# One expert stage gets another block order, and one entry of the load list becomes a barrier

## The chip, the cores and the metric

The kernel runs on one core of one Trainium2 chip. The metric is device time in microseconds (us), the median of several executions. One execution is also recorded by the hardware profiler; all rows below are from that one.

## The reference

The kernel computes a three-layer network on 256 tokens of width 1024, batch 1, all in float32. Layer one takes the tokens and 256 context tokens, mixes them by three kinds of attention and a gated linear scan, and ends in a mixture of experts: a router gives each token two of 32 experts, each with an up projection 1024 to 1024 (gate and value), a product with a sigmoid-weighted unit, and a down projection 512 to 1024. Then follow two layers of another kind (latent attention, stick-breaking attention, pooling), each with 32 experts of hidden width 256.

```
order = jnp.argsort(expert)                      # layer one: tokens sorted by expert
...
hid = jax.nn.silu(a) * b * combine[:, g, :, None]  # layers two and three, all experts, most weights 0
y = y + jnp.einsum('nef,efd->nd', hid, w_down[g])
```

Only experts that got tokens have to be computed, so how many tokens an expert has is known only at run time. The weights of the expert of layer one that has the fewest tokens weigh as much as those of the fullest: 6 MB.

## The kernel before, in words

Everything that is large comes from HBM through a ring of 22 SBUF slots of 1 MB (`RING`, class `Stream`). The order of the loads is a list, `S.specs`, written once by `stream_first` and `stream_rest`. `pump` takes entries from its head and issues one DMA on SyncE's queue (line L335) for each free slot; it is called at each `release` of a slot. A load whose address depends on the routing (`piece`, `get`) is not issued before the routing of its stage is known (`routes`). For all but the two fullest experts the DMA carries a condition, so that ranks with no tokens move nothing. Within the expert stages 20 slots serve the stream; the other two hold the split activations `hu` and `lu`. From the last block of a stage on, six freed slots are kept back for the next stage (`S.reserve(6)`, five in the last one).

An expert stage (`moe_phase`) is cut into blocks of 128 rows. Its plan (`_plan`) has static blocks (fixed experts, whose loads need no routing: experts 8 to 11 in stage one, two to a block), and rank blocks, whose experts are sorted by token count at run time: rank 0 gets two blocks ("wide", 256 rows, one set of weights), rank 1 one block, then pairs of experts with 64 rows each, then quads of four experts with 32 rows each. Whatever the order of the blocks, ranks keep their capacity. In stage one of the kernel before the order is

```
static static | rank0 rank0 rank1 | pair pair | quad quad quad quad quad
```

A block of n experts takes 6n MB of weights (4 up, 2 down), the second rank-0 block none. All blocks take the same rows through TensorE: n experts occupy n column groups side by side. In each turn p the loop runs `up(p)` (L1700, eight steps over the width), a gather of the group of blocks after (odd p only), the scatter of block p-2, `down(p-1)` (L1700 too) and a transposition of block p (L1724). Up slots are freed as the steps go on, down slots at the end of `down`.

After the last block come some statistics (`stats`, L1807 to L1829), and then a nest of branches (`nest`, L1847): rare routings need spare blocks, which lie inside the branches. In the recorded execution none is taken. Every engine runs through the branch. Then the next layer (`second_phase`) scales the tokens (L1920), transposes them (L1929), copies them (L1933, L1935) and projects them with six weight blocks `win2` (L1954); `prep` first splits each block into two halves on ScalarE and VectorE (L1903, L1907). Its loads stand in the list right behind the stage's last expert: `fg` (after stage one only), `win2` block 0, the constants `c2`, `win2` block 1, `wuq2`, `wsm2`, `win2` blocks 2 to 5, the rest of `c2`, four of `wout2`.

Of the kernel before, what the change touches and what calls it, by code (L numbers as in the profile page):

```python
# [33 lines left out]
SPARE = 16  # L34
# [5 lines left out]
        self.width = 128 // n  # L40


def _plan(start, statics, wide, wides, pairs, quads):
    blocks = [Block("static", start + wide * i, wide) for i in range(statics // wide)]
    lead = len(blocks)
    rank = 0
    for halves in wides:
        blocks += [Block("rank", rank, 1, 128 * i) for i in range(halves)]
        rank += 1
    cap = [128 * h for h in wides]  # L50
    for n, m in ((2, pairs), (4, quads)):
        for _ in range(m):
            blocks.append(Block("rank", rank, n))
            rank += n
            cap += [128 // n] * n
    main = len(blocks)
    blocks += [Block("rank", rank + 2 * i, 2, spare=True) for i in range(SPARE // 2)]
    return start, statics, lead, blocks, main, rank, cap


PLAN = {1: _plan(8, 4, 2, (2, 1), 2, 5), 2: _plan(8, 8, 4, (), 4, 4)}


def _layout_columns():
# [12 lines left out]
def _consts_main():  # L77
# [13 lines left out]
    for k in (1, 2):  # L91
        st0, ns, lead, _, _, nr, cap = PLAN[k]
        static = (e >= st0) & (e < st0 + ns)
# [205 lines left out]
class Stream:  # L299
# [14 lines left out]
    def add(self, src, dst=None):  # L314
        self.specs.append((src, dst))

    def pump(self):
        while self.specs:
            src, dst = self.specs[0]
            if dst is not None:  # L320
                self.nc.sync.dma_start(dst, src)
                self.specs.pop(0)
                continue
            if not self.free:
                return
            if callable(src):
                src = src()
                if src is None:
                    return
            cond = None  # L330
            if isinstance(src, tuple):
                src, cond = src
            self.specs.pop(0)
            u = self.unit(self.free.pop(0))
            self.nc.sync.dma_start(u.t[:, :src.shape[1]], src, **({} if cond is None else {"cond": cond}))  # L335
            self.ready.append(u)
# [30 lines left out]
def _flat(ap):  # L367
    n = len(ap.shape)
    if n == 2:
        return ap  # L370
    names = "abcd"[:n - 1]
    return ap.rearrange(f"p {' '.join(names)} -> p ({' '.join(names)})")
# [3 lines left out]
def hybrid_kernel(ctx: ExitStack, tc: tile.TileContext, A, out, dbg=None):  # L376
# [11 lines left out]
    def mark(label):  # L388
        if dbg is not None and "_mark" in dbg:
            dbg["_mark"](label)  # L390

    S = Stream(nc, ringp, range(RING - LENT - 1))
# [33 lines left out]
            S.add(_flat(A["wout"][u]))  # L426

    routes = {}

    def expert(R, u):  # L430
        if u not in R.regs:
            R.regs[u] = nc.values_load(R.info[0:1, u:u + 1], engines=[ENG.SP], min_val=0, max_val=31)
        return R.regs[u]

    def piece(key, src, blk, i, sub):
# [4 lines left out]
        def get():  # L440
# [6 lines left out]
            if "n" not in R.regs:  # L447
                nr = PLAN[key[0]][5]
                R.regs["n"] = nc.values_load(R.info[0:1, nr + SPARE + 1:nr + SPARE + 2], engines=[ENG.SP], min_val=0,
# [4 lines left out]
    def add_moe(key, ups, dns, nu, nd):  # L454
        _, _, lead, blocks, NL, _, _ = PLAN[key[0]]

        def add(p, src, n):
            if blocks[p].at:
                return
            for i in range(n):  # L460
                for e in range(blocks[p].n):
                    S.add(piece(key, src, blocks[p], e, (i,)))

        for p in range(NL + 1):
            if p < NL:
                add(p, ups, nu)
            if p > 0 and p != lead:
                add(p - 1, dns, nd)
            if p == lead - 1:
                add(p, dns, nd)  # L470

    def stream_rest():
        add_moe((1, 0), A["up1"], A["dn1"], 4, 2)
        S.add(A["fg"][0].to_broadcast([128, 1024]))
        for l in range(2):
            for b in range(6):
                S.add(_flat(A["win2"][l, b]))
                if b == 0:
                    S.add(A["c2"][:, 0:1792])
                if b == 1:  # L480
                    S.add(_flat(A["wuq2"][l]))
                    S.add(A["wsm2"][l])
            S.add(A["c2"][:, 1792:])
            for u in range(4):
                S.add(_flat(A["wout2"][l, u]))
            add_moe((2, l), A["gu2"][l], A["dn2"][l], 2, 1)
        S.add(A["fg"][1].to_broadcast([128, 1024]))
# [294 lines left out]
    def first_phase():  # L782
        with ExitStack() as es:
# [11 lines left out]
                               (A["wr1"], wrk.rearrange("p k e -> p (k e)")),  # L795
                               (A["br"].to_broadcast([128, 108]), brow.rearrange("p l e -> p (l e)"))])
            stream_rest()
            S.pump()
            def c1c(n):
# [634 lines left out]
    def moe_phase(kind, l, R, final=None):  # L1434
        _, _, lead, blocks, NL, NR, _ = PLAN[kind]
        NS = NR + SPARE
# [5 lines left out]
        with ExitStack() as es:  # L1442
# [318 lines left out]
            for p in range(NL + 1):  # L1761
                g = p // 2
# [97 lines left out]
            nest(NL)  # L1860
            if final is not None:
                S.release(fgu)
            mark("final")
            R.lu = S.unit(R.lu.slot)
            R.vrt = vrt
# [346 lines left out]

    R = first_phase()
    R = moe_phase(1, 0, R, 0)
    for l in range(2):
        R = second_phase(l, R)
        R = moe_phase(2, l, R, 1 if l == 1 else None)
# [22 lines left out]
```

## Time and profile before

| | us |
|---|---|
| median of 3 runs | 1468.6 (1467.32 to 1471.26) |
| the profiled execution | 1466.8 |
| its span | 1465.0 |
| TensorE busy | 1244.6 (85%) |
| VectorE / ScalarE / GpSimd busy | 433.7 / 341.8 / 98.3 |
| the load queue | 458.04 MB, 77.0% of the DMA engines' span |

Busy time on TensorE includes matmuls that run one after another while their weights arrive, so its share does not say which stage is limited by TensorE and which by loads; that is read stage by stage. Stage one's expert blocks lie between 299 and 739 us, those of the two later layers between about 895 and 1097 and between about 1255 and 1452 us.

### The profile page before, as it was taken

How to read it: one execution, taken by the hardware profiler on the slowest of the kernel's cores; microseconds unless marked ns; L12 is line 12 of the kernel's file. 1: busy time of each engine (PE TensorE's matmuls, PEld its weight loads, DVE VectorE, ACT ScalarE, POOL GpSimd, SP SyncE). 2: the span in 40 equal slices, each digit the busy share in tenths (PEclk: the TensorE clock that was granted, in tenths of full speed). 3: DMA queues.
4: the chain of work that ended last, by engine and by line, in shares of the span. 5: the costliest groups of instructions: out<-in, count | busy, mean ns of one | idle time of the engine just before them, and what ended most of it. 6: DMA issues, size and time to landing. Idle time of an engine off the chain costs nothing. (4 is left out here: it accounts for less than half of the span.)

```text
span 1465.0 us, 18831 instructions
## 1 busy us (share of the span) xinstructions
PE 1244.6 (85%) x7278; PEld 670.7 (46%) x7278; DVE 433.7 (30%) x1026; ACT 341.8 (23%) x709; POOL 98.3 (7%) x87
## 2 busy tenths in 40 slices
PE   5999999899999876767729998998672999899775
PEld 3778774544543311211218854443122875444211
DVE  5365443522212100100135524221012543422102
ACT  4431344211111100100035522211012552121102
POOL 1262100000000000000011100000000210000000
PEclk9999999999999988998969999999995999999998
DMA  8644329787689999999981458999996244899995
GB/s 343 259 174 158 144 69 421 261 336 292 246 330 386 421 421 421 420 421 422 421 328 66 179 191 336 420 421 421 421 421 260 98 203 185 341 421 421 421 421 205
DMA packets 64544, 459.47 MB, mean 314 GB/s; under 512 B 7408, under 2 KB 7728, under 8 KB 9904
## 3 DMA queue, kind: packets, MB, share of 16 engines
q1 hardware_dynamic: 64432, 458.04, 77.0%
q8 instruction: 63, 1.03, 0.3%
q14 instruction: 49, 0.40, 0.1%
HBM read 466.40 MB, written 1.05 MB: 319 GB/s over the span
## 5 line engine op out<-in xcount | busy, mean ns | idle before, releaser
L1700 PE MATMUL up<-ring,xg 128*32 128x512 f32 (+2 forms) x2016 | 381.5, 632 | 74.6 <-DMA ring<-in_up_dram 38.1
L1700 PEld LDWEIGHTS up<-ring,xg 128*32 128x32 f32 (+2 forms) x2016 | 105.8, 125 | 319.0 <-issue 180.4
L1700 PE MATMUL mm<-ring,hdT 128*32 128x512 f32 (+2 forms) x1008 | 199.6, 627 | 35.9 <-DMA ring<-in_dn_dram 34.4
L564 PE MATMUL ps<-ring,ring 128*128 128x256 f32 (+1 forms) x960 | 143.1, 306 | 1.3 <-POOL ring L897 0.6
L564 PEld LDWEIGHTS ps<-ring,ring 128*128 128x128 f32 x960 | 128.1, 191 | 20.0 <-issue 5.4
L1716 DVE TENSOR_TENSOR hd<-hd,up 128x256 f32<-128x256 f32 (+1 forms) x32 | 16.6, 520 | 393.3 <-ACT hd L1715 393.3
L1700 PEld LDWEIGHTS mm<-ring,hdT 128*32 128x32 f32 (+2 forms) x1008 | 53.4, 125 | 160.6 <-issue 89.7
L1715 ACT ACTIVATE hd<-up 128x256 f32<-128x256 f32 (+1 forms) x32 | 14.8, 464 | 400.3 <-PE up L1700 400.3
L1954 PE MATMUL ps<-ring,ring 128*128 128x256 f32 x384 | 52.1, 301 | 28.5 <-DVE ring L1935 28.5
L1515 PEld LDWEIGHTS mm<-P,ring 128*128 128x128 f32 x512 | 67.8, 202 | 12.6 <-issue 11.0
L1515 PE MATMUL mm<-P,ring 128*128 128x256 f32 x512 | 71.7, 298 | 0.8 <-DVE xg L1525 0.3
L1954 PEld LDWEIGHTS ps<-ring,ring 128*128 128x128 f32 x384 | 50.9, 208 | 29.5 <-ACT ring L1933 29.3
L599 PE MATMUL mm<-ring,ring 128*128 128x512 f32 (+1 forms) x192 | 64.1, 487 | 0.0
L1746 DVE SCALAR_TENSOR_TENSOR yl<-mm,gt,yh 128x512 fp32r<-128x512 f32 x40 | 30.0, 751 | 102.7 <-ACT yh L1745 102.7
L1745 ACT ACTIVATE yh<-mm,gt 128x512 fp32r<-128x512 f32 x40 | 27.5, 687 | 105.5 <-PE mm L1700 105.5
L1740 DVE SCALAR_TENSOR_TENSOR mm<-mm,gt,gmod 128x512 f32<-128x512 f32 x24 | 18.2, 758 | 113.1 <-PE mm L1700 113.1
L1742 ACT ACTIVATE yh<-mm 128x512 fp32r<-128x512 f32 x24 | 14.3, 597 | 153.9 <-DVE mm L1740 153.9
L599 PEld LDWEIGHTS mm<-ring,ring 128*128 128x128 f32 x192 | 35.8, 190 | 23.7 <-issue 21.5
L1923 POOL TENSOR_SCALAR ring<-ring,fr 128x1024 f32<-128x1024 f32 x2 | 5.7, 2884 | 462.7 <-DVE ring L1920 462.7
L1903 ACT ACTIVATE ring<-ring 128x1024 fp32r<-128x1024 f32 x24 | 24.1, 1059 | 43.9 <-SPq L1847 43.8
L823 POOL TENSOR_TENSOR ring<-ring,ring 128x1024 fp32r<-128x1024 f32 x12 | 30.1, 2508 | 49.4 <-ACT ring L822 38.5
L1907 DVE TENSOR_TENSOR ring<-ring,ring 128x1024 fp32r<-128x1024 f32 x24 | 28.1, 1220 | 17.3 <-ACT ring L1903 17.3
(464 smaller groups left out, 1384.4 us busy)
## 6 DMA issues: line engine op xcount, KB each, us to landing
ring<-in_gu_dram SPq DMA_DIRECT2D x128, 1024.0 KB, 19.8
ring<-in_dn_dram SPq DMA_DIRECT2D x124, 1024.0 KB, 19.6
ring<-in_up_dram SPq DMA_DIRECT2D x120, 1024.0 KB, 18.5
ring<-in_wmod_dram SPq DMA_DIRECT2D x24, 1024.0 KB, 5.1
ring<-in_win_dram SPq DMA_DIRECT2D x24, 1024.0 KB, 11.8
ring<-in_wout_dram SPq DMA_DIRECT2D x12, 1024.0 KB, 17.3
ring<-in_c_dram SPq DMA_DIRECT2D x2, 896.0 KB, 13.4
ring<-in_wsm_dram SPq DMA_DIRECT2D x2, 784.0 KB, 14.6
```

The lines of the kernel that those rows point to most:

```text
L564: pe.matmul(out, lhsT=a, rhs=b, start=first and i == 0, stop=last and i == 2, skip_group_check=True)
L599: pe.matmul(po, lhsT=O.mixT[:, s, a * 128:(a + 1) * 128], rhs=O.w[2 * c + s // 4][:, s % 4, sl.start - 512 * c:sl.stop - 512 * c], start=( ...
L823: (pool if q else dve).tensor_sub(lo[:, sl], u.t[:, sl], hi[:, sl].bitcast(F32))
L1515: pe.matmul(o, lhsT=xx[:, a, dt * 128:(dt + 1) * 128], rhs=P[:, a], start=(k == 0), stop=(k == 3))
L1700: pe.matmul(out[w * e:w * e + w], lhsT=x_of(w * e, w * e + w), rhs=wt, start=start, stop=stop)
L1716: dve.tensor_mul(hd, hd, pu[:, hid:uw])
L1740: dve.scalar_tensor_tensor(pd, pd, s.gt, gmod[:, hf * 512:(hf + 1) * 512], op0=OP.mult, op1=OP.mult)
L1745: act.activation(yh, pd, AF.Copy, scale=s.gt)
L1746: dve.scalar_tensor_tensor(yl, pd, s.gt, yh.bitcast(F32), op0=OP.mult, op1=OP.subtract)
L1903: act.activation(hi[:, sl], u.t[:, sl], AF.Copy)
L1907: dve.tensor_sub(lo[:, sl], u.t[:, sl], hi[:, sl])
L1954: pe.matmul(p[:, f * 256:(f + 1) * 256], lhsT=w[pw][:, dt, f * 128:(f + 1) * 128], rhs=hT[ph][:, dt], start=(i == 0 and f == 0 and dt == 0 ...
```

## The change

The plan takes the number of quads that go ahead of the wide blocks (`early`) and behind the pairs (`late`); ranks and capacities stay as they are. Stage one gets three early and two late quads:

```
static static | quad quad quad | rank0 rank0 rank1 | pair pair | quad quad
```

The other stages have none early and keep their order. The stream gets `gate()`: an entry of the list at which `pump` stops until it is opened. One stands in the list of each of the two later layers behind `win2` block 0 and the first part of `c2`. It is opened behind the branch nest of the stage before, and then `pump` runs.

```diff
-def _plan(start, statics, wide, wides, pairs, quads):
-    blocks = [Block("static", start + wide * i, wide) for i in range(statics // wide)]
-    lead = len(blocks)
-    rank = 0
-    for halves in wides:
-        blocks += [Block("rank", rank, 1, 128 * i) for i in range(halves)]
-        rank += 1
-    cap = [128 * h for h in wides]
-    for n, m in ((2, pairs), (4, quads)):
-        for _ in range(m):
-            blocks.append(Block("rank", rank, n))
-            rank += n
-            cap += [128 // n] * n
+def _plan(start, statics, wide, early, wides, pairs, late):
+    lead = statics // wide
+    cap = [128 * h for h in wides] + [64] * (2 * pairs) + [32] * (4 * (early + late))
+    rank = len(wides) + 2 * pairs
+    quads = [Block("rank", rank + 4 * i, 4) for i in range(early + late)]
+    blocks = [Block("static", start + wide * i, wide) for i in range(lead)] + quads[:early]
+    for r, halves in enumerate(wides):
+        blocks += [Block("rank", r, 1, 128 * i) for i in range(halves)]
+    blocks += [Block("rank", len(wides) + 2 * i, 2) for i in range(pairs)] + quads[early:]
     main = len(blocks)
...
-PLAN = {1: _plan(8, 4, 2, (2, 1), 2, 5), 2: _plan(8, 8, 4, (), 4, 4)}
+PLAN = {1: _plan(8, 4, 2, 3, (2, 1), 2, 2), 2: _plan(8, 8, 4, 0, (), 4, 4)}
...
+    def gate(self):
+        g = Unit()
+        g.shut = True
+        self.specs.append((g, None))
+        return g
+
     def pump(self):
         while self.specs:
             src, dst = self.specs[0]
+            if isinstance(src, Unit):
+                if src.shut:
+                    return
+                self.specs.pop(0)
+                continue
...
                 if b == 0:
                     S.add(A["c2"][:, 0:1792])
+                    barriers.append(S.gate())
...
             if final is not None:
                 S.release(fgu)
+            if final != 1:
+                barriers.pop(0).shut = False
+            S.pump()
```

## Rows read from the trace of the kernel before

**Rows 1.** The page's second part: GB/s moved in 40 equal slices of the span.

```profile
GB/s 343 259 174 158 144 69 421 261 336 292 246 330 386 421 421 421 420 421 422 421 328 66 179 191 336 420 421 421 421 421 260 98 203 185 341 421 421 421 421 205
```

**Rows 2.** Busy times by window in stage one; last columns granted clock, DMA share, GB/s.

```profile
313.62:730.01 416.39, 352.24 (x1814) 130.12 (x1810) 59.58 (x112) 39.54 (x68) 0.00 (x0) 0.94 0.93 382
500.00:730.00 230.00, 167.03 (x896) 44.20 (x888) 17.95 (x29) 12.66 (x21) 0.00 (x0) 0.90 1.01 421
350.00:370.00 20.00, 20.00 (x70) 8.74 (x69) 3.21 (x5) 2.14 (x4) 0.00 (x0) 1.00 0.38 152
```

**Rows 3.** Timeline of SyncE, 313 to 369 us: start, duration, DMA issues merged.

```profile
313.62 3.07 SPq L335 DMA_DIRECT2D ring<-in_up_dram  x4
...
343.25 2.94 SPq L335 DMA_DIRECT2D ring<-in_up_dram  x4
...
366.44 1.05 SPq L335 DMA_DIRECT2D ring<-in_up_dram  x2
```

**Rows 4.** Timeline of weight loads on TensorE: up steps of the last two quads.

```profile
634.13 0.16 PEld L1700 LDWEIGHTS up<-ring,xg 128*32 128x32 f32 x8 [2.35 <-DMA ring<-in_up_dram]
...
644.07 0.16 PEld L1700 LDWEIGHTS up<-ring,xg 128*32 128x32 f32 x8 [2.35 <-DMA ring<-in_up_dram]
...
687.05 0.16 PEld L1700 LDWEIGHTS up<-ring,xg 128*32 128x32 f32 x8 [2.34 <-DMA ring<-in_up_dram]
...
694.50 0.16 PEld L1700 LDWEIGHTS up<-ring,xg 128*32 128x32 f32 x8 [2.35 <-DMA ring<-in_up_dram]
```

**Rows 5.** Timeline of TensorE's matmuls, wide blocks and first pair of stage one.

```profile
368.56 13.90 PE L1700 MATMUL up<-ring,xg 128*128 128x512 f32 x32
...
388.74 7.13 PE L1700 MATMUL mm<-ring,hdT 128*128 128x512 f32 x16
...
396.14 13.90 PE L1700 MATMUL up<-ring,xg 128*128 128x512 f32 x32
...
419.13 13.95 PE L1700 MATMUL up<-ring,xg 128*64 128x512 f32 x64
```

**Rows 6.** Timeline at the end of stage one: the last down projection.

```profile
730.01 5.34 PE L1700 MATMUL mm<-ring,hdT 128*32 128x512 f32 x44 [1.41 <-DMA ring<-in_dn_dram]
```

**Rows 7.** Timeline behind stage one: next layer's loads, its first transpositions, splits, projection.

```profile
738.46 25.69 SPq L335 DMA_DIRECT2D ring<-in_wout_dram  x4
...
752.86 3.77 PE L1929 MATMUL ps<-cm,ring 128*128 128x128 f32 x16 [13.79 <-DVE ring L1920]
...
763.64 2.00 ACT L1903 ACTIVATE ring<-ring 128x1024 fp32r<-128x1024 f32 x2 [18.83 <-SPq L1847]
765.54 3.01 ACT L1933 ACTIVATE ring<-ps,vecs 128x256 fp32r<-128x256 f32 x8
...
767.42 7.85 PE L1954 MATMUL ps<-ring,ring 128*128 128x256 f32 x47 [10.79 <-DVE ring L1935]
```

**Rows 8.** The branch's line behind stage one: duration ns, first and last start.

```profile
L1847 SPq EVENT_SEMAPHORE  x9: 17/17/17, 748.4 to 763.7; - x9
L1847 PEldq COMPARE_BRANCH  x1: 6217/6217/6217, 738.6 to 738.6; - x1
...
L1847 ACTq EVENT_SEMAPHORE  x1: 17/17/17, 750.6 to 750.6; - x1
```

**Rows 9.** Timeline behind the second stage: transpositions, split, projection.

```profile
1107.05 3.76 PE L1929 MATMUL ps<-cm,ring 128*128 128x128 f32 x16 [10.18 <-DVE ring L1920]
...
1124.76 2.00 ACT L1903 ACTIVATE ring<-ring 128x1024 fp32r<-128x1024 f32 x2 [24.99 <-SPq L1847]
...
1128.54 6.70 PE L1954 MATMUL ps<-ring,ring 128*128 128x256 f32 x35 [17.73 <-DVE ring L1935]
```

**Rows 10.** The branch's line behind the second stage.

```profile
L1847 SPq EVENT_SEMAPHORE  x9: 17/17/17, 1110.8 to 1124.6; - x9
```

**Rows 11.** The branch's line behind the last stage.

```profile
L1847 SPq EVENT_SEMAPHORE  x7: 17/17/17, 1440.2 to 1446.6; - x7
...
L1847 PEldq COMPARE_BRANCH  x1: 3304/3304/3304, 1451.7 to 1451.7; - x1
```

More of the change, by code (lines that the diff above doesn't have):

```diff
@@ L40, in __init__ @@
         self.width = 128 // n
-def _plan(start, statics, wide, wides, pairs, quads):
-    blocks = [Block("static", start + wide * i, wide) for i in range(statics // wide)]
-    lead = len(blocks)
-    rank = 0
-    for halves in wides:
-        blocks += [Block("rank", rank, 1, 128 * i) for i in range(halves)]
-        rank += 1
-    cap = [128 * h for h in wides]
-    for n, m in ((2, pairs), (4, quads)):
-        for _ in range(m):
-            blocks.append(Block("rank", rank, n))
-            rank += n
-            cap += [128 // n] * n
+def _plan(start, statics, wide, early, wides, pairs, late):
[7 more added lines that the diff above has]
+    blocks += [Block("rank", len(wides) + 2 * i, 2) for i in range(pairs)] + quads[early:]
     main = len(blocks)
-    blocks += [Block("rank", rank + 2 * i, 2, spare=True) for i in range(SPARE // 2)]
-    return start, statics, lead, blocks, main, rank, cap
-PLAN = {1: _plan(8, 4, 2, (2, 1), 2, 5), 2: _plan(8, 8, 4, (), 4, 4)}
+    blocks += [Block("rank", len(cap) + 2 * i, 2, spare=True) for i in range(SPARE // 2)]
+    return start, statics, lead, blocks, main, len(cap), cap
+PLAN = {1: _plan(8, 4, 2, 3, (2, 1), 2, 2), 2: _plan(8, 8, 4, 0, (), 4, 4)}
 def _layout_columns():
@@ L428, in hybrid_kernel @@
     routes = {}
+    barriers = []
     def expert(R, u):
```

## The prediction

> **What bounds the kernel now.** The page's busy shares come first and settle nothing: TensorE's 85% is a mean over stages. The slices of GB/s do more [rows 1]. The expert stages show rows of 420 to 422, and nothing in the kernel exceeds that, so there the load queue is the limit. Between them the rate falls as far as 66: those stretches wait for engines. In stage one, slices 11 to 13 (246, 330 and 386; one slice is 36.6 us) stand just ahead of seven at 420 to 422. So the same stage first leaves the queue partly idle and then waits for it.
>
> The windows put numbers on that. From the first routed load's issue at 313.62 to the last wait for a down weight at 730.01 the mean is 382 GB/s; in 500 to 730 it is 421; in 350 to 370 it is 152 while TensorE is busy for all of the 20 us [rows 2]. SyncE's timeline gives the reason: 16 routed units of 1 MB are issued between 313.62 and 346.2, the next at 366.44 [rows 3]. All 20 slots were taken by then, and rank 0's units stay until its second block is done. The second part of the stage is the reverse: a step of a quad's up projection comes every 9.94 us (634.13 to 644.07), four units of 2.485 us, and TensorE waits each time [rows 4].
>
> Between stages the wait is another one. Behind stage one ScalarE's split starts at 763.64 after 18.83 us of waiting for SyncE at the branch, behind the second stage at 1124.76 after 24.99 [rows 7, 9]. SyncE's nine semaphore steps at the branch end at 763.7 and 1124.6 [rows 8, 10]. I read them as waits for the landings of what SyncE has issued: they end as `wout2`, the last thing ahead of the branch in the list, comes in.
>
> **The order, part by part.** The change moves work and adds none: the same 12 blocks, the same DMAs, registers loaded as before (the first four quad ranks and the rank count now at once, one 0.8 us step each by the pace of four issues in 3.07 us [rows 3], beside transfers of 2.485 us each, so hidden).
>
> How much can it give? The routed stream took 416.39 us at 382 GB/s; its bytes at 421 take 416.39 x 382 / 421 = 377.8. That leaves 38.6 us of idle queue [rows 2]. By units: 26 ranks of 6 units are 156, but the last quad's steps come every 7.45 us (687.05 to 694.50), three units, so one rank has no tokens [rows 4] and 150 units x 2.485 = 372.8, which leaves 43.6. These are the upper bounds.
>
> What idle time remains? With the stream at full rate from about 314.6, unit k lands at 314.6 + 2.485k. The first 16 slots come free as before, from the static blocks [rows 3]. Then the early quad frees four slots in every quarter of its up projection (13.9 / 4 = 3.5 us [rows 5]; a quad's matmuls run side by side, so I give it a wide block's time) while four units need 9.94: no shortage. Three quads and rank 0's up weights are 76 units, landed at 503.5. The third quad's down then ends about 5.3 us to 7 later [rows 6, 5], near 510. From there five wide or pair blocks run at TensorE's pace, 27.6 and 23.0 us in turn (368.56 to 396.14 to 419.13 [rows 5]). The second rank-0 down ends near 561, the first pair's down near 611. Just ahead of each the ring is fullest: at 561, 80 routed units are free again, so 100 may be out, and unit 100 lands at 563; at 611, 100 are free, and unit 120 lands at 613. So the queue is just supplied, twice with 2 us to spare. I charge 1 us of restart each. If each of the five blocks came 2 us late, the queue would lose 10. The bounds of this part are thus 28 and 43; I take 38.6 - 2, about 37, since the rate by bytes is the one measured over this very stretch.
>
> Then the late quads. TensorE would be at the last up projection near 635 while its weights (unit 136) land at 653: the end is again set by the queue, as before, and the step behind it too (5.34 us of matmuls after the last wait [rows 6]). Nothing else comes late: TensorE's own chain would end near 671 (635, 13.9 of up, two downs of 7.1 and their scatters), some 20 us ahead of the loads.
>
> **The barrier, part by part.** Ahead of the branch remain `win2` block 0, part of `c2` and, after stage one, `fg`; 11 loads go behind it. SyncE then has only about 2.4 MB, 6 us, of landings to wait for behind the last down weight. Since the last landing comes ahead of 5.3 us of matmuls, the final scatter and the statistics, SyncE is through before ScalarE needs it. The last stage shows this state: with only `fg` ahead of its branch, SyncE's steps end at 1446.6, and TensorE gets to its branch at 1451.7 [rows 11]. So SyncE doesn't wait for the other engines there.
>
> What is late next? ScalarE's own passage (750.6 [rows 8]), then the transpositions, which start at 752.86 and are not moved by this part [rows 7]. A quarter of them (0.9 us) gives ScalarE its first copy; from the first copy to the first projection matmul it took 767.42 - 765.54 = 1.9 us, and the copies now follow transpositions of 3.77 us where they took 3.01 alone, say 0.6 more [rows 7]. 752.86 + 0.9 + 1.9 + 0.6 = 756.3 in place of 767.42: 11.1 us. Behind the second stage the same sum is 1107.05 + 3.4 = 1110.4 in place of 1128.54: 18.1 us [rows 9]. Together 29.2.
>
> The cover for the late loads: in terms of the last down landing (730.0 before, L), SyncE passes at about L + 6, and TensorE's projection starts at L + 26. `win2` block 1 is needed one block later (47 matmuls in 7.85 us [rows 7]), L + 34. It lands at L + 11, and even if SyncE had to wait for TensorE's passage (738.6 + 6.2 = 744.8 [rows 8], L + 15) at about L + 20; block 2 stands three entries further, L + 27, needed at L + 42. Each block needs 7.85 us and each unit 2.485, so the distance grows. Behind stage two the last matmuls come sooner after the last landing, but the order of needs is the same. The queue has nothing else to carry then, as before: 66 GB/s in the slice that follows [rows 1].
>
> Nor are these gains lost later: the static loads of the next stage wait for slots that the layer's own end frees, so they start earlier by as much.
>
> The bounds of this part: zero, if SyncE stays the last at the branch; above, the branch itself. TensorE's branch takes 6.2 us with the queue full of loads and 3.3 with it quiet [rows 8, 11]; if it is quiet at both, 2.9 x 2, about 6 us more. I take no gain from that, since SyncE may restart the queue before the others branch. The Trainium skill ("Runtime: NRT & Kernel Launch", Instruction fetch mechanics) says that a taken branch to code outside the fetched pages has to wait until a DMA has brought it. By that rule the branch's own stall outlives the barrier. The trace agrees: 6.2 and 3.3 us on TensorE's branch [rows 8, 11].
>
> **The sum.** Profiled execution 1466.8, less 37, less 29.2: 1400.6. The median of the runs shown is 1.8 above that execution, so 1402.
>
> **The rivals.** (1) The barrier gives nothing: SyncE, or the loads that now come late, hold ScalarE as long as before. For it: the steps at the branch are 15.3 us long [rows 8], and I infer what they wait for. Against: the last stage [rows 11]. 1402 + 29 = 1431. (2) The idle queue only moves: rank 0's six slots are held for two blocks in the new place too, and the ring is nearly full twice. Then the queue stands still as it did in 350 to 370 [rows 2], and only the barrier counts: 1402 + 37 = 1439. Against: those blocks now start with the ring nearly empty. (3) Slower: the 11 loads reach the queue late. If SyncE issues them x us after TensorE could have used the first, each of the two layers stands x longer; the change is lost when 2x exceeds 66, x over 33; at x = 36 the time is 1474. For it: 25 us were seen at this place [rows 9]. Against: the distances above are positive. (4) No change, by gains and such a stall in balance: 1469.
>
> **How the numbers follow.** The forecast 0.68, (1) 0.12, (2) 0.12, (3) 0.04, (4) 0.04. A measurement of this kernel can tell 0.3%, 4.4 us, from no change. Faster takes the forecast, (1) and (2): 0.92; same 0.04; slower 0.04. The forecast's own range is 1402 - 6 (43 in place of 37) - 6 (quiet branches), 1390, to 1402 + 9 (28 in place of 37) + 3, 1414. To hold 8 in 10 the range has to take in (1): 1390 to 1432.
>
> **What would show it.** Right: GB/s at 421 from about 315 to 695 in stage one without the 152 at 350 to 370; the last wait for a down weight near 693; ScalarE's wait for SyncE at the branch gone, the first projection matmul 26 us behind the last down landing (37 before) and 3.4 us behind the first transposition (14.6 before). Wrong: waits of SyncE for slots between 550 and 620 with the rate falling; TensorE or ScalarE waiting for `win2` blocks; TensorE behind the queue at the last quads.

## The result and the profile after

The changed kernel takes 1411.4 us (median of 4 runs, 1409.2 to 1411.53) against 1467.96 for the kernel before (4 runs). The ratio is 0.9611, 95% interval 0.9587 to 0.9636. The profiled execution has a span of 1409.8 us, 55.2 less than before. Line numbers have moved: L1700 is now L1709, the branch L1856, the split L1915, the scaling L1932, the transpositions L1941, the projection L1966.

Stage one first. The windows of the changed kernel, from the first routed issue to the last wait for a down weight, and three stretches in it (last columns: granted clock, DMA share, GB/s):

```profile
318.57:698.70 380.13, 331.15 (x1812) 127.92 (x1809) 59.41 (x110) 38.89 (x67) 0.00 (x0) 0.96 1.01 419
318.57:325.00 6.43, 5.88 (x46) 2.79 (x44) 2.31 (x8) 1.20 (x2) 0.00 (x0) 1.00 0.86 302
350.00:370.00 20.00, 18.68 (x146) 6.30 (x140) 2.18 (x6) 1.69 (x3) 0.00 (x0) 1.00 1.02 421
550.00:620.00 70.00, 70.00 (x356) 33.66 (x358) 16.65 (x30) 10.29 (x18) 0.00 (x0) 1.00 1.01 420
```

The routed stream takes 380.13 us where it took 416.39 [rows 2]: 36.3 less. The 152 GB/s at 350 to 370 have become 421. In 550 to 620, where TensorE is busy all the time with the wide blocks and pairs, the queue runs at 420: both are full at once. Clearly slower is only the start of the stream (302 GB/s in the first 6.43 us). In SyncE's own waits there, the slots are the tight spot that the ledger showed, and they cost no rate:

```profile
SPq L342 <- PE mm L1709: 29.3, 6, 10.9
SPq L342 <- PE up L1709: 20.7, 10, 3.4
```

Then the way through the first branch, in the timeline (the counterpart of [rows 6, 7]):

```profile
698.70 5.34 PE L1709 MATMUL mm<-ring,hdT 128*32 128x512 f32 x44 [2.07 <-DMA ring<-in_dn_dram]
...
705.74 0.35 SPq L342 DMA_DIRECT2D ring<-in_win_dram  x1
...
719.75 2.00 ACT L1915 ACTIVATE ring<-ring 128x1024 fp32r<-128x1024 f32 x2 [6.25 <-ACTq L1856]
725.82 1.67 DVE L1932 TENSOR_SCALAR ring<-ring,fr 128x512 f32<-128x512 f32 x4 [11.37 <-issue]
726.45 3.77 PE L1941 MATMUL ps<-cm,ring 128*128 128x128 f32 x16 [18.68 <-DVE ring L1932]
...
729.87 12.65 PE L1966 MATMUL ps<-ring,ring 128*128 128x256 f32 x96
```

and the branch's line in the same stretch (duration ns, first and last start; [rows 8] before):

```profile
L1856 SPq EVENT_SEMAPHORE  x9: 17/17/17, 697.0 to 705.6; - x9
...
L1856 PEldq COMPARE_BRANCH  x1: 6757/6757/6757, 707.3 to 707.3; - x1
...
L1856 DVEq EVENT_SEMAPHORE  x1: 21/21/21, 720.8 to 720.8; - x1
```

SyncE is through at 705.6, ahead of every other engine, and issues the held loads at 705.74. ScalarE waits only for its own branch. VectorE is through at 720.8, but its first instruction starts at 725.82, 5.0 us later, after a wait that the profile can name only as "issue". TensorE's first projection matmul comes at 729.87, 31.2 us behind the last wait for a weight (37.4 before).

Behind the second stage (the counterpart of [rows 9]) there is no such gap. The projection comes 20.1 us behind the last wait, where it came 1128.54 - 1090.27 = 38.3 us behind it:

```profile
1054.27 3.62 PE L1709 MATMUL mm<-ring,hdT 128*32 128x512 f32 x26 [0.18 <-DMA ring<-in_dn_dram]
...
1070.34 1.67 DVE L1932 TENSOR_SCALAR ring<-ring,fr 128x512 f32<-128x512 f32 x4 [5.97 <-DVEq L1856]
1070.42 2.01 ACT L1915 ACTIVATE ring<-ring 128x1024 fp32r<-128x1024 f32 x2 [6.63 <-DMA ring<-in_win_dram]
...
1074.39 5.80 PE L1966 MATMUL ps<-ring,ring 128*128 128x256 f32 x38
```

ScalarE and VectorE are both through their branch at 1070.1 here, and their rows above start 0.3 and 0.2 us later. So ScalarE's wait ends with its branch, although its row names a load.

The account of the 55.2 us, by these landmarks: first phase 5.0 more (first routed issue 318.57, was 313.62), stage one 36.3 less, first branch 6.2 less, from the projection to the next stage's last wait 1.5 more, second branch 18.2 less, the rest 1.0 less.

Two things were to be tested: whether the two parts are worth what the account says, each alone, and what the 5.0 us of VectorE and the 5.0 us of the first phase are.

### The profile page after: what moved, and what is told of

Read it like the earlier page. It is cut to its first block, busy times and chain, and to the rows that moved or that the text cites. A ratio compares the mean times of both kernels' runs of the same rounds, so it can differ in the third digit from the quotient of the medians.

```text
span 1409.8 us, 18827 instructions
## 1 busy us (share of the span) xinstructions
PE 1233.2 (87%) x7278; PEld 673.1 (48%) x7278; DVE 434.2 (31%) x1024; ACT 342.8 (24%) x709; POOL 98.3 (7%) x87
## 5 line engine op out<-in xcount | busy, mean ns | idle before, releaser
L1709 PE MATMUL up<-ring,xg 128*32 128x512 f32 (+2 forms) x2016 | 370.9, 626 | 64.7 <-DMA ring<-in_gu_dram 36.6
L1709 PEld LDWEIGHTS up<-ring,xg 128*32 128x32 f32 (+2 forms) x2016 | 104.2, 124 | 298.7 <-issue 180.5
L1709 PE MATMUL mm<-ring,hdT 128*32 128x512 f32 (+2 forms) x1008 | 193.9, 633 | 26.4 <-DMA ring<-in_dn_dram 24.5
L1709 PEld LDWEIGHTS mm<-ring,hdT 128*32 128x32 f32 (+2 forms) x1008 | 53.4, 125 | 145.1 <-issue 89.2
L1749 DVE SCALAR_TENSOR_TENSOR mm<-mm,gt,gmod 128x512 f32<-128x512 f32 x24 | 18.2, 759 | 102.8 <-PE mm L1709 102.8
L1966 PE MATMUL ps<-ring,ring 128*128 128x256 f32 x384 | 49.8, 292 | 0.0
L1966 PEld LDWEIGHTS ps<-ring,ring 128*128 128x128 f32 x384 | 48.7, 198 | 0.2
L1941 PE MATMUL ps<-cm,ring 128*128 128x128 f32 x32 | 7.5, 426 | 28.8 <-DVE ring L1932 28.8
```

What stands on the lines that cost most here:

```text
L1709: pe.matmul(out[w * e:w * e + w], lhsT=x_of(w * e, w * e + w), rhs=wt, start=start, stop=stop)
L1749: dve.scalar_tensor_tensor(pd, pd, s.gt, gmod[:, hf * 512:(hf + 1) * 512], op0=OP.mult, op1=OP.mult)
L1966: pe.matmul(p[:, f * 256:(f + 1) * 256], lhsT=w[pw][:, dt, f * 128:(f + 1) * 128], rhs=hT[ph][:, dt], start=(i == 0 and f == 0 and dt == 0 ...
```

## The experiments

All were timed against the kernel before (1468 us).

**Order alone.** The diff takes the barrier out:

```diff
-                    barriers.append(S.gate())
...
-            if final != 1:
-                barriers.pop(0).shut = False
-            S.pump()
```

> The new block order without the barrier entries. Theory (the two parts add): between the first routed issue and the last landing in stage one 36 us less than before, as in the changed kernel; the waits for SyncE at the two branches stay (first projection matmul 37 to 38 us behind the last wait for a down weight); 1468 - 36 = 1432, or 1437 if the 5 us that the first phase lost in the changed kernel come with the new order. Rival (the order pays only with the barrier): 1445 or more.

Measured: 1433.03, ratio 0.9748 (0.9725 to 0.9771). The first routed issue is at 317.00, the last wait for a weight at 696.65: 379.7 us. SyncE still ends its branch steps with the landing of `wout2`, and ScalarE still waits for it:

```profile
696.65 5.34 PE L1708 MATMUL mm<-ring,hdT 128*32 128x512 f32 x44 [1.36 <-DMA ring<-in_dn_dram]
...
724.04 1.67 DVE L1928 TENSOR_SCALAR ring<-ring,fr 128x512 f32<-128x512 f32 x4 [11.64 <-issue]
...
730.22 2.00 ACT L1911 ACTIVATE ring<-ring 128x1024 fp32r<-128x1024 f32 x2 [18.76 <-SPq L1855]
...
734.00 14.32 PE L1962 MATMUL ps<-ring,ring 128*128 128x256 f32 x96 [5.56 <-DVE ring L1943]
```

The projection starts at 734.00, 37.4 us behind the last wait, as before. The order doesn't need the barrier. VectorE's late start is here too (its branch ends at 718.7), hidden behind ScalarE's wait, so the barrier is not what brings it.

**Barrier alone.** The diff:

```diff
-PLAN = {1: _plan(8, 4, 2, 3, (2, 1), 2, 2), 2: _plan(8, 8, 4, 0, (), 4, 4)}
+PLAN = {1: _plan(8, 4, 2, 0, (2, 1), 2, 5), 2: _plan(8, 8, 4, 0, (), 4, 4)}
```

> The old block order with the barrier entries. Theory: 18 us less behind stage two, and 11 us less behind stage one; 1468 - 29 = 1439. If the 5 us that VectorE waited behind its branch in the changed kernel belong to the barrier itself (loads that run again while the engines fetch), 6 and 18: 1444. Rival (the barrier does nothing for the old order): 1468.

Measured: 1444.4, ratio 0.9829 (0.9809 to 0.9848). VectorE starts at its branch's end (758.5), and the projection 27.9 us behind the last wait:

```profile
734.84 7.04 PE L1709 MATMUL mm<-ring,hdT 128*32 128x512 f32 x44 [2.56 <-DMA ring<-in_dn_dram]
...
758.72 1.67 DVE L1932 TENSOR_SCALAR ring<-ring,fr 128x512 f32<-128x512 f32 x4 [6.44 <-DVEq L1856]
...
762.77 7.50 PE L1966 MATMUL ps<-ring,ring 128*128 128x256 f32 x57
```

So the first branch gives 37.4 - 27.9 = 9.5 here. The 1.6 that are missing to 11.1 are about what the last matmuls took longer, 7.04 us in place of 5.34 [rows 6]; the mean granted clock was 0.79 in 734 to 742, with a part of it at the lower level, 1.2 GHz. The profiled execution's first phase is 4.4 us longer than before (first routed issue at 318.05), with the old order.

**The barrier opened later.** SyncE first stores a piece of VectorE's first result behind the branch into the output, where the final result overwrites it; only then does it issue the loads. So the queue is quiet while the engines go through:

```diff
                     dve.tensor_scalar(blk(xn, a, hf), blk(X.t, a, hf), R.vrt[a][-1][1], None, op0=OP.mult)
+                    if a == hf == 0:
+                        nc.sync.dma_start(out[0:1, 0:512], xn[0:1, 0, 0:512])
+                        barriers.pop(0).shut = False
+                        S.pump()
```

> The changed kernel, but the barrier opens only once VectorE's first scaling behind the branch is done: SyncE first stores 2 KB of that result into the output (overwritten at the end), then issues the loads. Theory (the loads that run again slow the other engines' passage: 5 us before VectorE's first instruction at the first branch, and branches of 6.3 to 6.8 us on TensorE in place of 3.3): VectorE starts at its branch's end, TensorE's branch takes about 3.3 us; 1411 - 5 - 3 - 3 = 1400. Rival 1 (the 5 us have another cause): 1405 to 1411. Rival 2 (the loads now come too late for the projection's second block): 1411 or more, with waits for win2 blocks.

Measured: 1400.63, ratio 0.9545 (0.9523 to 0.9567), below the changed kernel's interval. At the first branch:

```profile
L1856 PEldq COMPARE_BRANCH  x1: 3557/3557/3557, 704.4 to 704.4; - x1
...
L1856 DVEq EVENT_SEMAPHORE  x1: 21/21/21, 715.2 to 715.2; - x1
```

```profile
717.79 1.68 DVE L1929 TENSOR_SCALAR ring<-ring,fr 128x512 f32<-128x512 f32 x4 [6.21 <-issue]
...
721.84 8.39 PE L1967 MATMUL ps<-ring,ring 128*128 128x256 f32 x58
```

TensorE's branch takes 3.6 us in place of 6.8, VectorE's late start shrinks from 5.0 to 2.6 but stays, and the projection comes 27.4 us behind the last wait at the first branch, 17.6 at the second. Against the changed kernel that is 3.8 + 2.5 = 6.3 us of the 12.1 between the two profiled spans (1397.7 and 1409.8); another 4.5 are the first phase, which was short in this execution (first routed issue at 314.03). A fairer pair is the repeat of the changed kernel (the last run below): its first phase was as short (314.05), its last matmuls of the stage took as long (6.64 us, here 6.71), and its span is 1407.0. Against it the late barrier gains 9.3, of which the branches give 33.5 - 27.4 = 6.1 and 20.1 - 17.6 = 2.5.

**VectorE's instructions shifted.** 32 tiny ones more, far ahead of the branch:

```diff
             mark("moe")
+            if kind == 1:
+                pad = wx.tile([32, 1], F32, name="pad")
+                for _ in range(32):
+                    dve.memset(pad, 0.0)
```

> The changed kernel with 32 more tiny VectorE instructions (memset of 32x1) ahead of the first block of stage one. Theory (VectorE's 5 us behind the first branch are a fetch whose place depends on where its instructions fall): the 5 us vanish or move elsewhere, 1406 if they fall beside other work. Rival (they are a wait of another kind, tied to that instruction): the 5 us stay, 1411 to 1413.

Measured: 1406.49, ratio 0.9576 (0.9555 to 0.9597). VectorE now starts at its branch's end:

```profile
L1860 DVEq EVENT_SEMAPHORE  x1: 21/21/21, 723.1 to 723.1; - x1
```

```profile
699.21 7.04 PE L1713 MATMUL mm<-ring,hdT 128*32 128x512 f32 x44 [1.90 <-DMA ring<-in_dn_dram]
...
723.30 1.67 DVE L1936 TENSOR_SCALAR ring<-ring,fr 128x512 f32<-128x512 f32 x4 [6.65 <-DVEq L1860]
...
727.13 3.07 PE L1970 MATMUL ps<-ring,ring 128*128 128x256 f32 x19
```

The projection comes 27.9 us behind the last wait, as with the barrier alone. The late start depends on where VectorE's instructions fall in its program, not on what the instruction waits for. With the run before it (2.6 us where the queue is quiet, 5.0 where it is full) that is what a fetch of instructions over the DMA engines would do.

The DMA view counts instruction packets by the time at which they start. In the changed kernel, in 723.7 to 723.9, one starts 2.0 us ahead of VectorE's late instruction (725.82). In the late barrier, in 715.7 to 715.9, one starts 2.0 us ahead of it again (717.79). The changed kernel's row comes first, here and below:

```profile
q14 instruction: 1, 0.01, 10.2%
```

```profile
q14 instruction: 1, 0.01, 17.2%
```

All six profiles with a late start have such a packet 2.0 us ahead. Here, where VectorE isn't late, none starts between 721.2 and its first instruction. The branch itself looks alike. A larger instruction packet starts in 711.6 to 711.8 in the changed kernel, some 4.4 us behind the start of TensorE's branch, and in 705.4 to 705.6 in the late barrier, some 1.0 us behind it:

```profile
q8 instruction: 1, 0.02, 30.4%
```

```profile
q8 instruction: 1, 0.02, 36.0%
```

TensorE's branch ends 2.4 and 2.5 us behind the packet's start. So the time that the loads add passes before the packet starts. The view doesn't say which engine a packet is for; that these are VectorE's and TensorE's is read from the times.

**One early quad in place of three, and five.** The diffs are `_plan(8, 4, 2, 1, (2, 1), 2, 4)` and `_plan(8, 4, 2, 5, (2, 1), 2, 0)`.

> The changed kernel with one quad ahead of the wide blocks and four behind. Theory (the wide blocks need only start with an empty ring and a busy queue; one quad drains the ring as well as three): the same ledger shifted, the queue at 421 GB/s through the stage, 1411 to 1416. Rival (each early quad is worth a third of the order's 36 us): 1411 + 24 = 1435.

Measured: 1414.44, ratio 0.963 (0.9614 to 0.9646). Windows of this kernel:

```profile
318.39:702.41 384.02, 334.38 (x1812) 128.97 (x1808) 59.45 (x110) 38.84 (x67) 0.00 (x0) 0.96 1.00 414
450.00:470.00 20.00, 20.00 (x86) 7.96 (x85) 4.25 (x7) 2.28 (x4) 0.00 (x0) 1.00 0.86 336
```

```profile
446.86 7.13 PE L1709 MATMUL mm<-ring,hdT 128*128 128x512 f32 x16
```

One quad does nearly all of it. The 3.9 us that it lacks are where the ring is full for a moment (336 GB/s), at the first of the two tight spots: the row at 446.86 is the down projection of the second rank-0 block.

> The changed kernel with all five quads ahead and none behind. Theory (the stage ends by the loads only as long as TensorE has less work left than the queue): the last quad's down would end near 619, and rank 0's second block, rank 1, the pairs and their downs, some 106 us of TensorE's own pace, end near 725 in place of 704: 1411 + 21, less up to 5 for quieter branches, 1427 to 1432. Rival (only the queue's total counts, the order of loads does not): 1411.

Measured: 1434.16, ratio 0.9768 (0.9751 to 0.9784). That is 2 us above the range expected. The stage's last routed load is issued at 687.6. From 700 to 720 the queue moves only 159 to 220 GB/s, part of it for the next layer, and TensorE works on until 732.9:

```profile
690.00:730.00 40.00, 39.26 (x164) 16.16 (x166) 7.58 (x11) 5.80 (x9) 0.00 (x0) 1.00 0.71 279
```

```profile
617.99 7.07 PE L1709 MATMUL mm<-ring,hdT 128*32 128x512 f32 x64
...
725.83 7.09 PE L1709 MATMUL mm<-ring,hdT 128*64 128x512 f32 x32
```

The last quad's down ends at 625 (expected near 619: I had left out that it waits behind the next block's up and gathers), and from there the rest takes 108 us (106 expected).

**Late barrier and shifted instructions together.**

> The barrier opened behind VectorE's first scaling (as in the run before that did so), and the 32 tiny VectorE instructions too. Theory (VectorE's late start is a fetch set by where its instructions fall; 2.6 us of it were left with the queue quiet): it starts at its branch's end, 1400.6 - 2.6 = 1398. Rival (the rest of the wait belongs to the late opening): 1400 to 1401.

Measured: 1399.92 (1397.63 to 1406.48), ratio 0.9529 (0.9513 to 0.9545). The median can't be told from the 1400.63 of the late barrier alone; the trace can tell. VectorE starts 0.2 us behind its branch, and the projection, at 726.25, is 25.3 us behind the last wait at 700.95:

```profile
L1860 DVEq EVENT_SEMAPHORE  x1: 21/21/21, 722.0 to 722.0; - x1
```

```profile
722.20 1.67 DVE L1933 TENSOR_SCALAR ring<-ring,fr 128x512 f32<-128x512 f32 x4 [3.81 <-DVEq L1860]
...
726.25 3.99 PE L1971 MATMUL ps<-ring,ring 128*128 128x256 f32 x22
```

Its first phase was the longest of all (first routed issue at 320.37, 6.3 us later than in the late barrier alone), which is most of why the profiled span, 1404.7, doesn't show the gain.

**The changed kernel once more.**

> The changed kernel once more, for the first phase alone: the first routed issue came at 313.6 us in the kernel before, at 318.6 in the changed one, and at 314.0 to 318.7 in four variants. Theory (the first phase varies from execution to execution): it comes anywhere in 313 to 319, other than 318.6 by more than 1 us. Rival (it is set by the program): 318.6 within 0.5.

Measured: 1409.51 (2 runs). First routed issue in the changed kernel, the first time and this time:

```profile
318.57 4.34 SPq L342 DMA_DIRECT2D ring<-in_up_dram  x4
```

```profile
314.05 15.27 SPq L342 DMA_DIRECT2D ring<-in_up_dram  x10
```

The same program has both. The first phase's length belongs to the execution, not to the change. VectorE's late start is there again (718.8 to 723.91, 5.1 us).

The first branch was worth less this time: the projection comes 33.5 us behind the last wait, where it came 31.2 behind it.

```profile
694.39 6.64 PE L1709 MATMUL mm<-ring,hdT 128*32 128x512 f32 x44 [2.06 <-DMA ring<-in_dn_dram]
...
727.86 12.19 PE L1966 MATMUL ps<-ring,ring 128*128 128x256 f32 x96
```

The last matmuls took 6.64 us at a mean granted clock of 0.80, where they took 5.34 at 1.00, and VectorE's branch 6.7 in place of 5.6.

## Why the prediction was right, and where a size was off

- **What bounds the kernel.** Right. Stage one was held by an idle queue early and a full one late; the bytes moved at full rate gave the new length: 378 + 2 predicted, 380.1 measured (379.7 to 380.6 in five more profiles with three early quads).
- **The order.** 37 predicted, 36.3 measured, and 36 as a kernel of its own. The ledger of the ring held: two tight moments, no loss of rate with three quads, 3.9 us with one. The step that TensorE would again wait for the last quads held as well. Its limit showed with five early quads, where TensorE's own chain ends the stage. That 37 came out so closely is in part luck: the two restarts that were charged, 1 us each, don't show (420 GB/s in 550 to 620), and the start of the stream (302 GB/s for 6.43 us), which was not charged in this sum, costs 1.8.
- **The barrier behind stage two.** 18.1 predicted, 18.2 measured. SyncE's steps were waits for landings, as inferred; with two loads ahead of the branch (three behind stage one) it is through first.
- **The barrier behind stage one.** 11.1 predicted, 6.2 measured, 3.9 in the repeat. The mis-sized term is "the transpositions, which start at 752.86 and are not moved by this part": VectorE's scaling ahead of them starts 5.0 us late, because in the new order its program has a stall just behind the branch, by the packets above a wait for instructions. Without that the same branch gives 9.5, in the barrier alone and in the new order with 32 instructions more.
- **Quiet branches.** No gain was taken, because SyncE might restart the queue first. It does, 705.74 against 707.3 for TensorE's branch. The late barrier shows what that costs: 3.8 and 2.5 us, 6.1 and 2.5 against the repeat. At the first branch about 2.5 of it is VectorE's shorter late start.
- **The late loads.** No `win2` block was late in the changed kernel. With the barrier opened later still, ScalarE waits for one, 1.7 and 0.9 us.
- **The sum.** 66.2 predicted for the profiled pair, 55.2 found: 4.9 are VectorE's stall, 5.0 the first phase, which the rows of one execution couldn't show to vary; 1.1 are spread over the rest. In medians 56.6; the two parts as kernels of their own gave 35.8 and 24.4, 3.6 more together. That fits the stall: the order alone hides it behind ScalarE's wait, and the barrier alone doesn't have it.

Of the rivals, (1) and (2) fall with the two kernels that carry one part each; (3) and (4) with the result.

## What to carry to other kernels

When a stage has blocks that are limited by loads and blocks that are limited by TensorE, their order decides whether the two limits overlap: put a load-limited block first so that the ring is empty when the compute-limited ones begin, and keep enough loads for the end that TensorE isn't left working alone. A queue that waits at a branch for all that it has issued should have little issued there; and loads that restart while the engines are still on their way through the branch lengthen that way.

## What had not been expected of the hardware

- An engine's first instruction behind a branch can start 5.0 us after the branch's end with the load queue full, 2.6 with it quiet, and at once when 32 instructions more stand ahead of it in its program. An instruction packet starts 2.0 us ahead of each such late start.
- TensorE's branch took 5.9 to 6.8 us with loads running and 3.3 to 3.8 with the queue quiet. Its instruction packet started 3.5 to 4.5 us behind the branch's start with loads running, some 1.0 in the two kernels with the late barrier.
- The first phase of the same program took 314.05 us in one execution and 318.57 in another, to the first routed issue; over all profiled kernels it ranged from 313.62 to 320.37. Changes of 5 us can't be read from one profiled pair at that place.
